# Transposing the gate's columns later, and scaling the first groups at a layer border on one engine

## The chip, the cores and the metric

The kernel runs on one core of a Trainium2 chip. The metric is device time in microseconds (us) of one execution, median of three runs. TensorE (PE) multiplies matrices into eight PSUM banks, VectorE (DVE) and ScalarE (ACT) work element by element, POOL (GpSimd) here issues a few transfers and computes a few powers, SP issues the loads. Each engine takes its instructions strictly in the order of the program; between engines only semaphores order the work.

## The reference

A trunk of two layers on x (256 tokens, 2048 columns), all float32:

```python
cond = silu(c)
for i in range(2):
    mod = cond @ mod_w[i] + mod_b[i]
    shift, scale, gate = split(mod, 3)
    h = rms_norm(x, norm_w[i]) * (1.0 + scale) + shift
    y = mixer(h) @ w_out          # layer 0 ("A"): dilated windows, three head groups; layer 1 ("B"): causal blocks
    x = x + gate * y
return rms_norm(x, final_norm_w)
```

Each mixer projects h with a large weight matrix (10 x 2048 columns in A, 4 x 2048 in B), runs attention over 16 heads and multiplies by silu of a part z.

## The kernel before, in words

**Products.** A float32 product is done in three passes of a faster format: every operand is split into a high and a low half, and high x high, high x low and low x high are added in PSUM. The activations are split once (tiles hA, hB, yA, yB: index 0 the high half, index 1 the low one). Weights arrive in units of 128 x 1024 (512 KB) in one of five raw tiles; `convert` (L337) issues the load on SP and has ScalarE write the high half wh (L347), and `finish_converts` (L351) has VectorE write the low half wl (L353). Four units fit in the ring of converted tiles; a few more are "held" in other tiles around the border.

**Order.** The order of the work is written out by hand as a list of steps. A step is one call that emits matmuls. `at_once(i, f)` puts f right behind the matmuls of step i; then `finish_converts` emits the low halves of all converted units that still lack them; then come the conversions planned for the step (`plan_conversions`, L357: a unit converts at the step that frees its buffer, and no earlier than eight steps ahead of its first use); then what `at(i, f)` put there:

```python
    for i, (n, pe) in enumerate(steps):
        pe()
        for f, a in first_tasks.get(i, []):
            f(*a)
        finish_converts()
        for m in plan.get(i, []):
            convert(m)
        for f, a in tasks.get(i, []):
            f(*a)
```

**Parts.** The projections run by parts of 512 columns (four heads), 8 units each. A part with the weights stationary (`whole_part`, L535) has twelve steps: four head steps for units 0 and 1 (called h0 to h3 in the text), one step each for units 2, 3, 4 and 5, and four head steps for units 6 and 7, after each of which a head is moved from PSUM by ScalarE and VectorE (L547, L548). In a head step and in every second step the low-half products (L302) and the high ones (L297) change order. Behind the last head of a part z ScalarE also takes the silu, with a table load (L550).

**The gate.** The vector `mod` is computed by VectorE, 512 columns of `mod_w` at a time (`mod_unit`, L135, L143: multiply by cond and sum), spread over the steps by `add_pieces` (L171). For the gate third of a layer (part 2) it ends with `gate_write` at step i1 + 1, where i1 is the step after the last piece: `mod_sums` (L149) adds four partial sums for each of 16 columns, TensorE transposes the 16 columns (L161) into a PSUM bank (ps_y), ScalarE copies them (L163), POOL writes them to DRAM (L164). `gate_read` at i1 + 3 has POOL read them back, spread over all partitions, into the tiles `gate` (L169). In both layers i1 is the first step, h0, of the part behind a part z.

**The border of the layers.** The out product of layer A ends with column group 3, first for token tile 0 (last step `mid`), then in eight more steps for tile 1 (last step `last`). Behind each of the two, `epilogue` (L679) gates and adds (L684, L686) and sums squares (L691) on VectorE, POOL takes the power (L703), and `norm_b` (L718) has VectorE write a diagonal (L721). `norm_transpose(tt, g)` (L723) then transposes four blocks of group g with the diagonal on TensorE (L728) and scales them: VectorE the first n blocks into hf (L736), ScalarE the others into hs (L738), with n = 3 for even g and 2 for odd g. `norm_split` (L741) writes the high halves on ScalarE (L194) and the low ones on VectorE (L195), one instruction each for hf and for hs. Groups 0 to 3 of tile 0 are transposed at steps mid + 3, 5, 9 and 11, those of tile 1 at last + 4, 5, 6 and 8. Layer B's first part starts at step last + 1 with units 0 to 3 (held) and needs group g from its units 2g and 2g + 1 on, tile 0 first. The conversions of its units 4 and 5 are planned at mid + 5 and mid + 6, so that their low halves come at mid + 6 and mid + 7, which are the steps last - 2 and last - 1.

Of the kernel before, what the change touches and what calls it, by code (L numbers as in the profile page):

```python
# [12 lines left out]
F32 = mybir.dt.float32  # L13
# [5 lines left out]
P = 128  # L19
# [34 lines left out]
def trunk_kernel(ctx: ExitStack, tc: tile.TileContext, x, c, small_w, mod_t, weights, final_norm_w, dmask, out, laid_out):  # L54
# [11 lines left out]
    tmpp = pool("tmpp", 1)  # L66
# [79 lines left out]
    def mod_sums(m, n, step=1):  # L146

        cols = slice(m, m + (n - 1) * step + 1, step)
        nc.vector.tensor_reduce(modc[:, cols], modq[:, cols], axis=AX.X, op=ALU.add)  # L149
# [5 lines left out]

    def gate_write(layer):

        mod_sums(48 * layer + 32, 16)
        scratch[layer] = dram.tile([KC, P], F32, name=f"gate_rows{layer}", tag=f"g{layer}")
        pt = ps_y.tile([P, 512], F32, name="pgt", tag="y")  # L160
        nc.tensor.transpose(pt[:KC, :P], modc[:, 48 * layer + 32:48 * layer + 48], ident)  # L161
        rows = small.tile([P, P], F32, name="grows", bufs=1)
        nc.scalar.activation(rows[:KC], pt[:KC, :P], AF.Copy)  # L163
        nc.gpsimd.dma_start(scratch[layer], rows[:KC])  # L164
# [6 lines left out]
    def add_pieces(i0, i1, layer, part):  # L171

        for n in range(32):
            at(i0 + n * (i1 - i0) // 32, mod_unit, layer, 16 * part + n // 2, n % 2)
        if part == 2:
            at(i1 + 1, gate_write, layer)
            at(i1 + 3, gate_read, layer)

    def scale_b():
        mod_sums(48, 32)  # L180
# [10 lines left out]
    def split(dst, src):  # L191

        hi = dst[:, :, 0]
        nc.scalar.activation(hi, src, AF.Copy)  # L194
        nc.vector.tensor_tensor(dst[:, :, 1], src, hi.bitcast(F32), op=ALU.subtract)  # L195
# [115 lines left out]
    def add_unit(w, u, n0, hold=None, after=-1):  # L311
        return add_halves([(w, 2 * u, n0), (w, 2 * u + 1, n0)], hold, after)
# [6 lines left out]
    def add_step(ns, pe):  # L319
        i = len(steps)  # L320
        steps.append((ns, pe))
        for n in ns if isinstance(ns, tuple) else (ns,):
            if units[n]["first"] is None:
                units[n]["first"] = i
            units[n]["last"] = i
        return i

    def at(i, f, *a):
        tasks.setdefault(i, []).append((f, a))

    def at_once(i, f, *a):

        first_tasks.setdefault(i, []).append((f, a))
# [17 lines left out]
    def finish_converts(c=slice(0, 2)):  # L351
        for raw, wh, wl in to_finish:
            nc.vector.tensor_tensor(wl[:, c], raw[:, c], wh[:, c].bitcast(F32), op=ALU.subtract)  # L353
        if c.stop == 2:
            to_finish.clear()
# [166 lines left out]
    def product(p, key, st, n, u, first, last):  # L522
        def pe():
            moving(group_ps(key), st, (2 * u, 2 * u + 1), conv[n], (0, 1), first, last)
        return add_step(n, pe)
# [58 lines left out]
    while min(done) < KC:  # L584
        n_ready = sum(r <= t for r in READY)
        n = done.index(min(done)) if n_ready < KC else next(i for i, d in enumerate(done) if d < KC)
# [18 lines left out]
    for k in range(1, KC):  # L605
        i0, i1 = READY[k - 1], READY[k]
# [8 lines left out]
    for j in range(1, 4):  # L615
# [4 lines left out]
        for n, p in enumerate(PARTS[EARLY:] if j == 1 else PARTS):  # L620
# [3 lines left out]
            for u in range(8):  # L624
                m = add_unit(wA, u, COL[p] * D + j * GC)
                i = product(p, ("A", j, p), st_a, m, u, u == 0, u == 7)
# [4 lines left out]
    for n, (layer, part) in enumerate(((0, 2), (1, 0), (1, 1))):  # L631
        add_pieces(*(span[0] + (n + k) * (span[1] - span[0]) // 3 for k in range(2)), layer, part)
# [3 lines left out]
    def out_steps(l, w, epilogue, hold):  # L636
        st = lambda kc: ys[l, kc // 4][:, kc % 4]

        def step(g, u, n=None, tts=(0, 1)):
            n = add_unit(w, u, g * GC) if n is None else n  # L640

            def pe():
                moving(group_ps(("o", l, g)), st, (2 * u, 2 * u + 1), conv[n], tts, u == 0, u == 7)
            return add_step(n, pe)

        b0 = len(steps)
        for g in range(2):
            for u in range(6):
                step(g, u)
        for u in (6, 7):  # L650
            for g in range(2):
                i = step(g, u)
                if u == 7:
                    at_once(i, epilogue, g, (0, 1))
        for u in range(8):
            i = step(2, u)
        at_once(i, epilogue, 2, (0, 1))
        b1 = len(steps) + 2
        both = 0 if hold else 4
        for u in range(both):  # L660
            step(3, u)
        ns = {u: add_unit(w, u, 3 * GC, HOLD[u] if hold and u < 4 else None, b0 + 12 if hold else -1) for u in range(both, 8)}
        for u in range(both, 8):
            mid = step(3, u, ns[u], (0,))
        for tt in range(2):
            at(b1, sums_before, tt)
        at_once(mid, epilogue, 3, (0,))
        for u in range(both, 8):
            i = step(3, u, ns[u], (1,))
        at_once(i, epilogue, 3, (1,))  # L670
        return b0, mid, i
# [7 lines left out]
    def epilogue(l):  # L679
        def f(g, tts):  # L680
            ps = groups["o", l, g]
            tmp = tmpp.tile([P, 2, GC], F32, name="tmp", tag="tmp")
            for tt in tts:
                nc.vector.tensor_tensor(tmp[:, tt], ps[tt], gate_of(g), op=ALU.mult)  # L684
            for tt in tts:
                nc.vector.tensor_tensor(X[g][:, tt], X[g][:, tt], tmp[:, tt], op=ALU.add)  # L686
                s = ssp[:, tt * 4 + g:tt * 4 + g + 1]
                if g < 3:
                    nc.scalar.activation(tmp[:, tt], X[g][:, tt], AF.Square, accum_out=s)
                else:  # L690
                    nc.vector.tensor_tensor_reduce(tmp[:, tt], X[g][:, tt], X[g][:, tt], 1.0 / D, ssb[:, tt:tt + 1],  # L691
                                                   ALU.mult, ALU.add, s)
        return f
# [12 lines left out]
    b0, mid, last = out_steps("A", "a_w_out", epilogue("A"), True)  # L706
# [7 lines left out]
    hB_box = []  # L714
# [8 lines left out]
    def norm_transpose(tt, g):  # L723
        if not hB_box:
            hB_box.append(hpool.tile([P, KC, 2, S], F32R, name="hB", tag="h"))
        pt = (ps_s, ps_o, ps_t, ps_y)[g].tile([P, 512], F32, name="pxt", tag="soty"[g])
        for b in range(4):
            nc.tensor.matmul(pt[:, b * P:(b + 1) * P], X[g][:, tt, b * P:(b + 1) * P], rB[tt], start=True, stop=True)  # L728
        hf = tp.tile([P, 4, P], F32, name="t")
        hs = tmpp.tile([P, 2, P], F32, name="hs", tag="tmp")  # L730
        n = 3 - g % 2
        for b in range(4):
            k = 4 * g + b
            src, a, s = pt[:, b * P:(b + 1) * P], abB[:, k:k + 1], modc[:, 48 + k:49 + k]
            if b < n:
                nc.vector.tensor_scalar(hf[:, b], src, a, s, op0=ALU.mult, op1=ALU.add)  # L736
            else:
                nc.scalar.activation(hs[:, b - n], src, AF.Identity, scale=a, bias=s)  # L738
        hfB[tt, g] = (n, hf[:, :n], hs[:, :4 - n])

    def norm_split(tt, g):  # L741
        n, hf, hs = hfB[tt, g]
        split(hB_box[0][:, 4 * g:4 * g + n, :, tt * P:(tt + 1) * P], hf)
        split(hB_box[0][:, 4 * g + n:4 * g + 4, :, tt * P:(tt + 1) * P], hs)

    for tt, i in enumerate((mid, last)):
        at_once(i, norm_b, tt)
        for g, n in enumerate((3, 5, 9, 11) if tt == 0 else (4, 5, 6, 8)):
            at_once(i + n, norm_transpose, tt, g)
            at(i + n, norm_split, tt, g)  # L750
# [3 lines left out]
    for j in range(4):  # L754
# [4 lines left out]
        for p in PARTS_B:  # L759
            col = COL_B[p] * D + j * GC  # L760
            if j == 0 and p == "v":
                ns = [add_unit(wB, u, col, HOLD[u] if u < 4 else None)
                      for u in range(8)]
                for tt in range(2):
                    for u, n in enumerate(ns):
                        def pe(n=n, u=u, tt=tt, key=("B", j, p)):
                            moving(group_ps(key), st_b, (2 * u, 2 * u + 1), conv[n], (tt,), u == 0, u == 7)
                        i = add_step(n, pe)
            elif p != "v":
                i = whole_part("B", j, p, st_b, wB, col)  # L770
                continue
            else:
                for u in range(8):
                    i = product(p, ("B", j, p), st_b, add_unit(wB, u, col), u, u == 0, u == 7)
# [4 lines left out]
    b0, mid, last = out_steps("B", "b_w_out", epilogue("B"), False)  # L779
# [56 lines left out]
    for i, (n, pe) in enumerate(steps):  # L836
        pe()
        for f, a in first_tasks.get(i, []):
            f(*a)
        finish_converts()  # L840
        for m in plan.get(i, []):
            convert(m)
        for f, a in tasks.get(i, []):
            f(*a)
# [38 lines left out]
```

## Time and profile before

| | before |
|---|---|
| median of three runs | 1584.31 us (1582.89 to 1584.82) |
| the profiled execution | 1584.17 us, span of its instructions 1582.1 us |
| mean granted clock of TensorE in the span | 0.994 |
| busy in the span | TensorE 1555.3 us, VectorE 1128.3 us, ScalarE 757.4 us, POOL 30.3 us |
| loads of weights | 512 of 512 KB, on SP's queue |

The span runs from the first to the last instruction; the 2.1 us outside it belong to start and end of the execution. A busy time is the sum of an engine's instructions; matmuls overlap, so a row of several matmuls ends later than the next row starts. "Idle before" is the time an engine stood before an instruction, with the instruction that released it. The granted clock is the share of full speed (2.4 GHz) that TensorE was given, 1.00 or 0.50 at any moment (2.4 or 1.2 GHz).

### The profile page before, as it was taken

How to read it: one execution, taken by the hardware profiler on the slowest of the kernel's cores; microseconds unless marked ns; L12 is line 12 of the kernel's file. 1: busy time of each engine (PE TensorE's matmuls, PEld its weight loads, DVE VectorE, ACT ScalarE, POOL GpSimd, SP SyncE). 2: the span in 40 equal slices, each digit the busy share in tenths (PEclk: the TensorE clock that was granted, in tenths of full speed). 3: DMA queues.
4: the chain of work that ended last, by engine and by line, in shares of the span. 5: the costliest groups of instructions: out<-in, count | busy, mean ns of one | idle time of the engine just before them, and what ended most of it. 6: DMA issues, size and time to landing. Idle time of an engine off the chain costs nothing. (4 is left out here: it accounts for less than half of the span.)

```text
span 1582.1 us, 23691 instructions
## 1 busy us (share of the span) xinstructions
PE 1555.3 (98%) x8960; PEld 1366.4 (86%) x8960; DVE 1128.3 (71%) x2008; ACT 757.4 (48%) x1041; POOL 30.3 (2%) x35
## 2 busy tenths in 40 slices
PE   8999999999999998999999999999999998999997
PEld 6898899999988887888888888888888887888886
DVE  7889887667678766777777775766448887465666
ACT  7644444445444544444544444554545455455542
POOL 4000000000000000000000000000000000000000
PEclk9999999999999999999999999999999999999999
DMA  9978997553788577888578886364467896645543
GB/s 347 344 284 312 317 314 266 189 170 128 236 301 281 187 237 269 303 289 294 205 242 285 294 303 225 129 239 147 135 211 245 295 325 226 213 173 200 187 172 108
DMA packets 104726, 380.77 MB, mean 241 GB/s; under 512 B 11650, under 2 KB 11810, under 8 KB 104356
## 3 DMA queue, kind: packets, MB, share of 16 engines
q1 hardware_dynamic: 102528, 372.95, 67.8%
q0 software_dynamic: 1504, 5.26, 1.0%
q8 instruction: 70, 1.15, 0.3%
q10 hardware_dynamic: 580, 1.06, 0.2%
q14 instruction: 44, 0.36, 0.1%
HBM read 377.10 MB, written 2.11 MB: 240 GB/s over the span
## 5 line engine op out<-in xcount | busy, mean ns | idle before, releaser
L347 ACT ACTIVATE wh<-raw 128x1024 fp32r<-128x1024 f32 (+1 forms) x505 | 527.3, 1056 | 519.1 <-PE acc L297 174.1
L353 DVE TENSOR_TENSOR wl<-raw,wh 128x1024 fp32r<-128x1024 f32 (+1 forms) x505 | 609.0, 1221 | 192.3 <-ACT wh L347 190.8
L297 PE MATMUL acc<-hA,wh 128*128 128x512 f32 x1152 | 289.4, 393 | 0.0
L297 PEld LDWEIGHTS acc<-hA,wh 128*128 128x128 f32 x1152 | 207.8, 189 | 36.7
L297 PE MATMUL acc<-hB,wh 128*128 128x512 f32 x768 | 197.2, 396 | 0.0
L284 PE MATMUL acc<-hA,wh 128*128 128x256 f32 x640 | 182.8, 286 | 1.0 <-ACT hA L256 1.0
L285 PE MATMUL acc<-hA,wh 128*128 128x256 f32 x640 | 182.0, 284 | 0.6 <-DVE hA L262 0.6
L286 PE MATMUL acc<-hA,wl 128*128 128x256 f32 x640 | 181.8, 284 | 0.0
L302 PEld LDWEIGHTS acc<-hA,wl 128*128 128x128 f32 x1152 | 157.8, 191 | 11.8
L302 PE MATMUL acc<-hA,wl 128*128 128x256 f32 x1152 | 161.1, 283 | 0.0
L297 PEld LDWEIGHTS acc<-hB,wh 128*128 128x128 f32 x768 | 138.0, 189 | 23.9
L273 PE MATMUL acc<-wh,hA 128*128 128x512 f32 x384 | 156.0, 406 | 1.0 <-DVE hA L258 1.0
L275 PE MATMUL acc<-wh,hA 128*128 128x512 f32 x384 | 151.1, 394 | 0.4 <-DVE hA L262 0.4
L274 PE MATMUL acc<-wl,hA 128*128 128x512 f32 x384 | 150.6, 392 | 0.0
L143 DVE CUSTOM_DVE_ANT_0 raw<-raw,cb 128x512 f32<-128x512 f32 x198 | 131.1, 689 | 18.4 <-DMA raw<-in_mod_t_dram 18.4
L284 PEld LDWEIGHTS acc<-hA,wh 128*128 128x128 f32 x640 | 123.5, 193 | 1.4 <-ACT hA L256 1.2
L285 PEld LDWEIGHTS acc<-hA,wh 128*128 128x128 f32 x640 | 123.6, 193 | 1.0 <-DVE hA L262 0.8
L286 PEld LDWEIGHTS acc<-hA,wl 128*128 128x128 f32 x640 | 123.5, 193 | 0.0
L302 PEld LDWEIGHTS acc<-hB,wl 128*128 128x128 f32 x768 | 106.0, 191 | 8.6 <-DVE wl L353 0.4
L302 PE MATMUL acc<-hB,wl 128*128 128x256 f32 x768 | 109.0, 284 | 0.2 <-DVE wl L353 0.2
L275 PEld LDWEIGHTS acc<-wh,hA 128*128 128x128 f32 x384 | 72.4, 189 | 17.1 <-DVE hA L262 1.3
L273 PEld LDWEIGHTS acc<-wh,hA 128*128 128x128 f32 x384 | 72.7, 189 | 15.9 <-ACT hf L259 2.2
(235 smaller groups left out, 1780.7 us busy)
## 6 DMA issues: line engine op xcount, KB each, us to landing
raw<-in_weights_dram SPq DMA_DIRECT2D x512, 512.0 KB, 4.4
raw<-in_mod_t_dram SPq DMA_DIRECT2D x132, 512.0 KB, 4.7
gate<-in_mod_t_dram SPq DMA_DIRECT2D x40, 512.0 KB, 5.3
dm<-in_mod_t_dram SPq DMA_DIRECT2D x20, 512.0 KB, 5.3
xin<-in_x_dram SPq DMA_DIRECT2D x2, 1024.0 KB, 6.2
gate<-gate_rows POOLq DMA_DIRECT2D x4, 512.0 KB, 6.9
x<-in_x_dram POOLq DMA_DIRECT2D x4, 512.0 KB, 6.4
fw<-in_final_norm_w_dram POOLq DMA_DIRECT2D x2, 512.0 KB, 4.7
```

Source lines behind the costliest of these rows:

```text
L143: nc.vector.tensor_tensor_reduce(part, part, cb[q], 1.0, 0.0 if q else mbT[:, m:m + 1], ALU.mult, ALU.add, modq[:, m, q:q + 1])
L273: nc.tensor.matmul(o, hi, wh[:, i], start=f, stop=False, skip_group_check=True)
L274: nc.tensor.matmul(o, hi, wl[:, i], start=False, stop=False, skip_group_check=True)
L275: nc.tensor.matmul(o, lo, wh[:, i], start=False, stop=l, skip_group_check=True)
L284: nc.tensor.matmul(o, wh[:, i, wc], hi, start=first and h % 2 == 0, stop=False, skip_group_check=True)
L285: nc.tensor.matmul(o, wh[:, i, wc], lo, start=False, stop=False, skip_group_check=True)
L286: nc.tensor.matmul(o, wl[:, i, wc], hi, start=False, stop=last, skip_group_check=True)
L297: nc.tensor.matmul(ps_of(h), ws[u][0][:, i, cols(h)], both, start=us[u] == 0 and i == 0, stop=low_first and us[u] == 7 and i == 1, skip_gr ...
L302: nc.tensor.matmul(ps_of(h)[:, 0:S], ws[u][1][:, i, cols(h)], st(2 * us[u] + i)[:, 0, :], start=False, stop=not low_first and us[u] == 7 a ...
L347: nc.scalar.activation(wh[:, c], raw[:, c], AF.Copy)
L353: nc.vector.tensor_tensor(wl[:, c], raw[:, c], wh[:, c].bitcast(F32), op=ALU.subtract)
```

## The change

The sums of the gate's columns stay at step i1 + 1. The transpose, the copy and the write move from i1 + 1 to i1 + 8, the read back from i1 + 3 to i1 + 10, in both layers. At the border, for groups 0 and 1 of tile 0, VectorE scales all four blocks, into one tile, and ScalarE none; the split is then one instruction on each engine. At the steps last - 2 and last - 1 no low halves are emitted; they follow at step `last`, behind the gating and the diagonal of tile 1.

```diff
     def gate_write(layer):
 
-        mod_sums(48 * layer + 32, 16)
         scratch[layer] = dram.tile([KC, P], F32, name=f"gate_rows{layer}", tag=f"g{layer}")
...
         if part == 2:
-            at(i1 + 1, gate_write, layer)
-            at(i1 + 3, gate_read, layer)
+            at(i1 + 1, mod_sums, 48 * layer + 32, 16)
+            at(i1 + 8, gate_write, layer)
+            at(i1 + 10, gate_read, layer)
...
         hf = tp.tile([P, 4, P], F32, name="t")
-        hs = tmpp.tile([P, 2, P], F32, name="hs", tag="tmp")
-        n = 3 - g % 2
+        n = 4 if tt == 0 and g < 2 else 3 - g % 2
+        hs = tmpp.tile([P, 2, P], F32, name="hs", tag="tmp") if n < 4 else hf
...
         split(hB_box[0][:, 4 * g:4 * g + n, :, tt * P:(tt + 1) * P], hf)
-        split(hB_box[0][:, 4 * g + n:4 * g + 4, :, tt * P:(tt + 1) * P], hs)
-
+        if n < 4:
+            split(hB_box[0][:, 4 * g + n:4 * g + 4, :, tt * P:(tt + 1) * P], hs)
+
+    late_low = range(last - 2, last)
...
-        finish_converts()
+        if i not in late_low:
+            finish_converts()
```

## Rows read from the trace of the kernel before

**Rows 1.** The page: busy us (share of the span) and instructions of each engine.
```profile
PE 1555.3 (98%) x8960; PEld 1366.4 (86%) x8960; DVE 1128.3 (71%) x2008; ACT 757.4 (48%) x1041; POOL 30.3 (2%) x35
```
**Rows 2.** Waits of TensorE, whole span: waiting, releaser, us, times, longest.
```profile
PE pgt L161 <- DVE modc L149: 9.0, 2, 4.8
...
PE acc L273 <- ACT hB L194: 1.2, 1, 1.2
...
PE acc L302 <- DVE wl L353: 0.2, 1, 0.2
```
**Rows 3.** Timeline of TensorE, first place: start, us, instruction, [idle before].
```profile
601.81 1.09 PE L297 MATMUL acc<-hA,wh 128*128 128x512 f32 x4
...
609.57 0.28 PE L161 MATMUL pgt<-ident,modc 128*16 128x128 f32 x1 [4.80 <-DVE modc L149]
...
614.99 3.82 PE L297 MATMUL acc<-hA,wh 128*128 128x512 f32 x16
...
630.75 1.09 PE L297 MATMUL acc<-hA,wh 128*128 128x512 f32 x4
...
637.33 3.82 PE L297 MATMUL acc<-hA,wh 128*128 128x512 f32 x16
```
**Rows 4.** Timeline of TensorE, second place.
```profile
1332.00 1.08 PE L297 MATMUL acc<-hB,wh 128*128 128x512 f32 x4
...
1344.56 3.82 PE L297 MATMUL acc<-hB,wh 128*128 128x512 f32 x16
...
1360.32 1.09 PE L297 MATMUL acc<-hB,wh 128*128 128x512 f32 x4
...
1366.89 3.82 PE L297 MATMUL acc<-hB,wh 128*128 128x512 f32 x16
```
**Rows 5.** Windows: length, busy of PE, PEld, DVE, ACT, POOL; granted clock, DMA share, GB/s.
```profile
609.60:613.60 4.00, 4.00 (x14) 3.33 (x15) 1.13 (x4) 0.57 (x2) 0.71 (x1) 0.57 0.79 260
1340.10:1344.00 3.90, 3.90 (x18) 3.47 (x17) 0.57 (x1) 1.85 (x2) 0.48 (x1) 0.56 0.42 151
...
617.00:624.00 7.00, 7.00 (x40) 6.08 (x40) 3.95 (x7) 3.19 (x3) 1.10 (x2) 1.00 0.95 310
```
**Rows 6.** Timeline of VectorE at the two places.
```profile
605.74 2.36 DVE L353 TENSOR_TENSOR wl<-raw,wh 128x1024 fp32r<-128x1024 f32 x2 [2.89 <-ACT wh L347]
...
609.30 0.22 DVE L149 TENSOR_REDUCE modc<-modq 128x16 f32<-128x64 f32 x1
...
1336.61 2.36 DVE L353 TENSOR_TENSOR wl<-raw,wh 128x1024 fp32r<-128x1024 f32 x2 [2.83 <-ACT wh L347]
```
**Rows 7.** The page: DMA issues, count, KB each, median us from issue to landing.
```profile
raw<-in_weights_dram SPq DMA_DIRECT2D x512, 512.0 KB, 4.4
...
gate<-gate_rows POOLq DMA_DIRECT2D x4, 512.0 KB, 6.9
```
**Rows 8.** Timeline of VectorE at the border.
```profile
1081.81 1.05 DVE L736 TENSOR_SCALAR t<-pxt,abB,modc 128x128 f32<-128x128 f32 x3 [0.64 <-PE pxt L728]
...
1084.82 0.56 DVE L195 TENSOR_TENSOR hB<-t,hB 128x384 fp32r<-128x384 f32 x1 [0.83 <-ACT hB L194]
...
1089.57 0.43 DVE L195 TENSOR_TENSOR hB<-t,hB 128x256 fp32r<-128x256 f32 x1 [1.08 <-ACT hB L194]
...
1090.25 2.35 DVE L353 TENSOR_TENSOR wl<-raw,wh 128x1024 fp32r<-128x1024 f32 x2
1092.52 0.68 DVE L684 TENSOR_TENSOR tmp<-acc,gate 128x512 f32<-128x512 f32 x1
...
1095.39 0.29 DVE L721 TENSOR_SCALAR diag<-ident,rstd 128x128 f32<-128x128 f32 x1 [0.66 <-POOL rstd L703]
...
1096.73 1.04 DVE L736 TENSOR_SCALAR t<-pxt,abB,modc 128x128 f32<-128x128 f32 x3
```
**Rows 9.** Timeline of TensorE at the border.
```profile
1089.33 0.39 PE L273 MATMUL acc<-held,hB 128*128 128x512 f32 x1
...
1098.81 0.50 PE L273 MATMUL acc<-wh,hB 128*128 128x512 f32 x1 [1.17 <-ACT hB L194]
```

## The prediction, made before the change was timed

> **What bounds the kernel now.** I read the page's busy times first: the matmuls fill 1555.3 of the 1582.1 us span, VectorE 71% and ScalarE 48% [rows 1]. So a change is worth what it takes from TensorE's order of work or adds to it, and the next view is the list of what TensorE waited for. The largest entry by far is 9.0 us in two waits, of 4.8 and (the rest) 4.2 us, of the gate's transposes for the sums of L149; the only wait at the border of the layers is 1.2 us for a high half of hB; low halves of weights (L353) cost 0.2 us in the whole span [rows 2]. The timeline of each place tells what a wait costs beyond its idle time, the granted clock tells why, and VectorE's timeline tells what was late.
>
> **Part 1: the transposes go seven steps later, the sums stay.** VectorE reaches the sums late because they are queued behind two low halves, which wait for ScalarE. At the first place these start at 605.74 and the sums at 609.30; at the second the low halves start at 1336.61 [rows 6]. TensorE, which is in order, stands at the transpose with ready heads behind it.
>
> What goes, first place. From the start of step h0 (601.81) to the first high product of unit 2 (614.99) are 13.18 us. The next part does the same work without the transpose from 630.75 to 637.33, in 6.58 us [rows 3]. So 6.60 us go: the 4.80 idle, 0.2 around the transpose, and 1.6 of slow products behind it, for the granted clock is 0.57 over the 4.00 us after the wait, which is full speed falling to the half level and back [rows 5]. Second place: 1332.00 to 1344.56 is 12.56 us, against 1360.32 to 1366.89, 6.57 [rows 4]: 5.99 us go, 4.2 of them idle, with the clock at 0.56 over 3.90 us behind it [rows 5]. Together 12.59 us, some 3.2 of which are clock.
>
> The Trainium skill ("TensorE: Matmul & The Clock Gate", section Terms) prices slow stretches by a rule: throttled time multiplied by one minus the granted share. By it the two stretches would cost 4.00 x 0.43 + 3.90 x 0.44 = 3.4 us and the whole sum would be 0.2 us larger. The trace is a little below that, as steps bound by something else lose less, and the measured difference stands in my sum.
>
> What takes its place. At the new step (i1 + 8, the first head step of units 6 and 7) PE's next wait could again be for the sums. Without the stall that step ends at about 604.6 + 2 x 1.4 + 4 x 2.8 + 1.4 = 620.0 (1.40 a head step, 2.8 a unit, from the spacing of [rows 3]); the sums are there by 609.5 [rows 6], ten us before. The transposes themselves still run: nothing to 0.28 us each (0.28 is the whole row [rows 3]; the next product started 0.04 behind it); I take 0.1, as matmuls overlap: 0.2 for both.
>
> What is late next: unit 2, whose low half is used first. First place: h2 and h3 now end at 607.4; the first of the two low halves, 1.2 us long, is done at 606.9 [rows 6]: no wait, 0.5 to spare. Second place: PE arrives at 1332.00 + 4 x 1.40 = 1337.6, the low half is done at 1336.61 + 1.2 = 1337.8, so a new wait of 0.25 us; the 0.2 us already in the waits is of this kind [rows 2]. Unit 3 comes 2.8 us after unit 2 and its low half 1.1. Units 4 and 5 convert once h3 has freed their buffers; those steps move forward with PE. Their loads are the doubt: SP issues a load when VectorE frees one of five raw tiles, and a load takes 4.4 us to land [rows 7]. Unit 5's raw tile is freed by unit 2's low half at 606.9, so it lands at about 611.4 and is converted by 613.6; PE wants it at 615.8. Unit 7's lands some 2.5 us after it and PE wants it at 618.6: a us or so to spare.
>
> Other queues moved past. ScalarE's copy of the transposed rows (L163) now sits between two evacuations of heads, where it idles; POOL's write and re-read have POOL's queue to themselves there, and the gate is read first by the gating of the out product, which for the first place is the row at 1092.52 and its kind, over 400 us later [rows 8]. I cost these at nothing; if their cover went, it would be DMA time, below as a rival. Part 1: 12.59 - 0.25 - 0.2 = **12.1 us**.
>
> **Part 2: the border.** TensorE waits 1.17 us at 1098.81 for the high half of group 2, tile 0 [rows 9]. That group was transposed early, but VectorE scales it only at 1096.73 [rows 8]: it was busy with low halves until 1092.52, then gating until the diagonal at 1095.39, then one more low half. Yet the last out product ended at 1089.33 [rows 9]. I place the new order in a row from 1081.81, in durations of [rows 8]: 4 scalings (1.05 / 3 each) 1.40, low half 1.2, one merged split of 512 columns 0.7 (0.56 for 384), low half 1.2, 4 scalings 1.4, low half 1.2, split 0.7: 1089.6. ScalarE's high halves come inside this, since it no longer has three scalings waiting for VectorE. The idle 0.83 and 1.08 us of VectorE at 1084.82 and 1089.57 are filled. So the gating starts at 1089.6 instead of 1092.52, 2.9 us earlier, and the diagonal at 1092.45. But then the two postponed low halves (2.27) run with the third one ahead of group 2: 1092.45 + (1096.73 - 1095.39) + 2.27 = 1096.06, only 0.7 us earlier. The wait shrinks from 1.17 to 0.5. The postponed halves themselves (units 4 and 5) are done at 1093.8 and 1094.9, and TensorE wants unit 4's just after 1098. What this part can do at most is remove 1.17; at worst the five us of extra or later VectorE work cost what they add, 3 x 0.35 = 1.05 less 0.2 of merged splits: 0.85 us lost. I take **+0.7**, because the idle that absorbs the added work is in the rows.
>
> **Sum.** 12.1 + 0.7 = 12.8 us off the profiled execution's 1584.17 (span 1582.1 and 2.1 around it), so 1571.4; the median of the three runs, 1584.31, is 0.14 above the profiled one, within their scatter of 1.9.
>
> **Rivals.**
> (a) *Weights late, once.* The gate's re-read is 2 x 0.5 MB and now falls in a busy stretch instead of behind a stall in which loads had got ahead. At 310 GB/s [rows 5] it takes 3.4 us of DMA time. If the first place passes that on to TensorE (a unit's spare time above is about 1 us), the result is 1571.4 + 3.4 = 1574.8. For: five raw tiles only, and 4.4 us to land. Against: from 617 to 624, where the re-read ran before, the DMA engines were 0.95 busy and TensorE 7.00 of 7.00 [rows 5]. At the second place the share was 0.42, so only one is counted. 12 in 100.
> (b) *Slower.* The same re-read, place i1 + 10, not sharing but going first: two issues of 6.9 us each [rows 7], 13.8 us without weights. With half of the four converted units in hand (2 x 2.8 us) TensorE would stand for 8.2 us, and lose 1.6 to the clock, at both places: 19.6 lost against 12.8 gained, about 1591. It decides once each place loses over 8 us. Against: again the stretch from 617 to 624. 2 in 100.
> The Trainium skill ("Trainium Kernel Development and Optimization", Key Constraints) speaks for (a) over (b): transfers issued from SP, ScalarE and POOL use the same 16 DMA engines and interleave. The trace agrees at 617 to 624, where both kinds were in flight and neither stopped TensorE.
> (c) *The change does not do what it says:* the moved transpose waits again, for its bank or a later VectorE instruction, as long as before. Then only the border is left: 1583.5. Against: the wait's releaser is L149 itself [rows 2]. 3 in 100.
> (d) *The clock falls anyway* at both places, although the idle is gone: 3.2 us less, 1574.6. Against: the drop is seen only behind the wait. 3 in 100.
>
> **The numbers.** The forecast has the other 80 in 100. Its own bounds: border wholly gone, no new wait and no cost of the transposes, clock by the rule, 0.5 + 0.25 + 0.2 + 0.2 better, less a us of scatter: 1569.4. At the other end the border loses 0.85 instead of gaining 0.7 and a us of scatter: 1574; (a) and (d) bring it to 1575.0. A difference under 0.2% (3.2 us) is about what a measurement of this kernel can't tell from none. Faster 0.95 (forecast, a, d), same 0.03 (c), slower 0.02 (b).
>
> **What would show it.** TensorE's waits without pgt, or under 0.1; L161 some 15 us behind L149; no half clock behind it; h0 to unit 2's high products 6.6 us at the first place, 6.8 at the second; a wait for a low half of some 0.25 at the second; at the border the gating at about 1089.6 and the wait for hB near 0.5. Wrong would be: new waits for wh or wl in the two parts behind the places (a, b), pgt still in the waits (c), a half clock without a wait (d), or a gating that starts past 1091.

## The result, and the profile after

The changed kernel takes 1573.1 us (median of four, 1571.62 to 1573.42) against 1584.31: a ratio of 0.9929, 95% interval 0.9912 to 0.9946. That is 11.2 us faster; 1571.4 was forecast, with a range of 1569.4 to 1575.0. The profiled execution took 1571.62 us, its span is 1569.6.

The page's first part, after (it answers to [rows 1]): TensorE's busy time fell by 4.9 us although it does the same matmuls, since fewer of them run at the half clock.

```profile
PE 1550.4 (99%) x8960; PEld 1361.2 (87%) x8960; DVE 1129.1 (72%) x2009; ACT 756.2 (48%) x1036; POOL 30.2 (2%) x35
```

TensorE's waits, after (to [rows 2]): pgt is gone from the list. A wait for a low half of 1.7 us is new, and the one for hB is 0.4 instead of 1.2.

```profile
PE acc L302 <- DVE wl L353: 1.7, 1, 1.7
...
PE acc L273 <- ACT hB L194: 0.4, 1, 0.4
```

TensorE's timeline at the first place, after (to [rows 3]): h0 starts at 600.11, unit 2's high products at 606.69, the moved transpose runs at 618.64 without a wait, and the new wait stands at 635.95.

```profile
600.11 1.09 PE L297 MATMUL acc<-hA,wh 128*128 128x512 f32 x4
...
606.69 3.82 PE L297 MATMUL acc<-hA,wh 128*128 128x512 f32 x16
...
615.91 1.97 PE L302 MATMUL acc<-hA,wl 128*128 128x256 f32 x12
617.72 1.09 PE L297 MATMUL acc<-hA,wh 128*128 128x512 f32 x4
618.64 0.27 PE L160 MATMUL pgt<-ident,modc 128*16 128x128 f32 x1
...
635.95 1.22 PE L302 MATMUL acc<-hA,wl 128*128 128x256 f32 x8 [1.67 <-DVE wl L353]
```

The same at the second place, after (to [rows 4]).

```profile
1324.97 1.08 PE L297 MATMUL acc<-hB,wh 128*128 128x512 f32 x4
...
1330.10 1.98 PE L302 MATMUL acc<-hB,wl 128*128 128x256 f32 x12
1331.91 3.82 PE L297 MATMUL acc<-hB,wh 128*128 128x512 f32 x16
```

From h0 to unit 2's high products are now 6.58 us (13.18 before) and 6.94 us (12.56 before): 6.60 and 5.62 us went. Windows of the kernel after show full speed behind the first place (to [rows 5]), and also at 97 us, where the profiled execution of before had a half clock:

```profile
606.00:620.00 14.00, 13.88 (x80) 11.94 (x79) 11.28 (x22) 5.94 (x8) 0.33 (x1) 1.00 0.92 310
...
97.00:101.00 4.00, 4.00 (x35) 4.00 (x35) 4.00 (x9) 1.06 (x1) 0.00 (x0) 1.00 0.91 325
```

The window of before for that stretch:

```profile
97.80:101.30 3.50, 3.50 (x19) 3.50 (x18) 3.25 (x7) 0.93 (x1) 0.00 (x0) 0.51 0.75 231
```

Nothing that runs there was changed, so 1.7 us of the two spans' difference belong to the two executions (h0 of the first place starts at 600.11 instead of 601.81). The 12.5 us between the spans are: 1.7 at the start, 6.60 and 5.62 at the two places, 0.73 at the border, less 1.67 for the new wait and 0.38 at 615.91, where twelve low-half products take 1.81 us to the next start instead of 1.43. These add up to 12.6, or to 12.3 with the new wait's price by distance (1.93, worked out at the end of the experiments). Without the start, about 10.8 us of the 12.5 are the change's, and the medians say 11.2.

VectorE's timeline at the border, after (to [rows 8]):

```profile
1075.91 1.37 DVE L736 TENSOR_SCALAR t<-pxt,abB,modc 128x128 f32<-128x128 f32 x4 [0.64 <-PE pxt L728]
...
1083.63 0.69 DVE L684 TENSOR_TENSOR tmp<-acc,gate 128x512 f32<-128x512 f32 x1 [0.47 <-PE acc L275]
...
1086.71 3.49 DVE L353 TENSOR_TENSOR wl<-raw,wh 128x1024 fp32r<-128x1024 f32 x3
1090.12 1.04 DVE L736 TENSOR_SCALAR t<-pxt,abB,modc 128x128 f32<-128x128 f32 x3
```

The gating starts 7.72 us behind the first scalings (10.71 before, [rows 8]), 3.0 us earlier, and group 2's scaling 14.21 behind them (14.92 before), 0.7 earlier. VectorE itself was ready 7.25 us behind the first scalings; it then stood 0.47 for the end of the last out product.

Where the new wait of 1.67 us comes from, in VectorE's timeline after: it stands 5.30 us at a load of `mod` columns (issued on SP at 625.76, so over 7 us on the way), and the low halves that TensorE waits for are queued behind it.

```profile
633.39 0.75 DVE L143 CUSTOM_DVE_ANT_0 raw<-raw,cb,smalls 128x512 f32<-128x512 f32 x1 [5.30 <-DMA raw<-in_mod_t_dram]
...
634.68 4.63 DVE L353 TENSOR_TENSOR wl<-raw,wh 128x1024 fp32r<-128x1024 f32 x4
```

And POOL's timeline after: the gate's re-read was issued at 625.07, just ahead of that load.

```profile
625.07 1.10 POOL L168 DMA_DIRECT2D gate<-gate_rows  x2 [4.69 <-DVE actA2q L548]
```

That is the prediction's rival (a) in kind, at about half its price. At the second place, where the re-read goes out too (POOL, 1347.95), no such wait came. The experiments ask whether the re-read is its cause (theory 1) or the loads run short there anyway (theory 2), what the clock costs, and which of the two border edits does the work.

### The profile page after: what moved, and what is told of

It is laid out like the page before. It is cut to its first block, busy times and chain, and to the rows that moved or that the text cites. A ratio compares the mean times of both kernels' runs of the same rounds, so it can differ in the third digit from the quotient of the medians.

```text
span 1569.6 us, 23684 instructions
## 1 busy us (share of the span) xinstructions
PE 1550.4 (99%) x8960; PEld 1361.2 (87%) x8960; DVE 1129.1 (72%) x2009; ACT 756.2 (48%) x1036; POOL 30.2 (2%) x35
## 4 chain that ended last, share of the span: by engine, by line
PE 91%; DVE 1%; DMA 1%; issue 0%; ACT 0%; POOLq 0%; POOL 0%; DVEq 0%; ACTq 0%
PE acc L297 27%; PE acc L302 14%; PE acc L273 11%; PE acc L275 11%; PE acc L274 10%; PE acc L285 4%; PE acc L286 4%; PE acc L284 4%; PE po L461 2%; PE pss L443 2%; PE pst L424 1%; DMA raw<-in_mod_t_dram 1%; PE po L494 1%; PE pss L478 1%; DVE wl L353 1%
```

## The experiments

Short diffs are against the changed kernel, or against the one before where that is said. Comparisons by profile are made by waits and distances, because whether and where a half clock falls in the first 100 us differs from execution to execution.

**The gate part alone.**

```diff
-        n = 4 if tt == 0 and g < 2 else 3 - g % 2
+        n = 3 - g % 2
...
-    late_low = range(last - 2, last)
+    late_low = range(0)
```

> The change with the border as it was before (scaling shared, low halves not postponed); the gate's transposes stay at i1 + 8. If the border part is worth the 0.7 us that the prediction gave it: the wait of the first products behind the border for hB is back at 1.1 to 1.2 us (0.44 with the whole change), everything at the two gate places as with the whole change (no pgt wait, one wait for a low half of about 1.7 us some 35 us behind the first place), time about 1573.8 us. If the border part is worth nothing: the wait stays near 0.4 and the time at 1573.1. If it did more than shorten that wait: over 1575.

Measured: 1573.04 us (ratio to before 0.9935, interval 0.9919 to 0.9951). TensorE's waits in this run:

```profile
PE acc L302 <- DVE wl L353: 2.0, 2, 1.8
PE acc L273 <- ACT hB L194: 1.2, 1, 1.2
```

The border's wait is back in full, as expected. Times can't tell 0.7 us here; the waits can. The new wait behind the first place (1.80, the longer of the two) comes with the gate part.

**The border part alone** (transposes at i1 + 1, read at i1 + 3, the rest as changed).

> The kernel before with the border part alone; the transposes stay at i1 + 1. If the parts are independent: pgt waits of 9.0 us as before, half clock behind both, the hB wait at 0.4 instead of 1.17, the gating of tile 1 within 0.3 us of the end of the last out product, span 0.7 us under before's (1581.4 where the clock does the same at the start). If the border is bound by something else: the hB wait above 0.9.

Measured: one run of 1581.9 us, span 1579.8; pgt 9.0 us in two waits, hB 0.44. The parts are independent. The span is 2.3 us under before's instead of 0.7, of which 1.7 lie ahead of the first place's stage (the first whole part starts at 404.8 us instead of 406.5; no half clock near 97 us in this execution either).

**Layer 0's gate read back later.**

```diff
-            at(i1 + 10, gate_read, layer)
+            if layer:
+                at(i1 + 10, gate_read, layer)
...
+    at(b0 + 3, gate_read, 0)
     at(b0 - 10, load_x, 0)
```

> The whole change, but layer 0's gate is read back only at the fourth step of the out product of layer A, some 360 us later, where no mod loads run. Theory 1, the re-read of 1 MB delays the loads (a mod load lands late, VectorE stands at it, the low half behind it is late): the wait of 1.7 us for a low half some 35 us behind the first place goes, all of it, no other wait above 0.5 us comes near the first place, the gate's sums and transposes as before; 1571.4 us. Theory 2, the loads run short behind the first place because the stall in which they got ahead is gone, re-read or not: a wait of over 1 us for a low half stays within 50 us behind the first place; 1573.1. If the out product has no room for the re-read: a new wait for a weight between steps b0 and b0 + 10.

Measured: 1570.66 us (1569.27 to 1571.5; ratio 0.992, interval 0.9902 to 0.9938). No wait for a low half is left in TensorE's whole list. In this kernel's timeline VectorE stands 2.10 us at the `mod` load instead of 5.30:

```profile
629.73 0.75 DVE L143 CUSTOM_DVE_ANT_0 raw<-raw,cb,smalls 128x512 f32<-128x512 f32 x1 [2.10 <-DMA raw<-in_mod_t_dram]
```

This is theory 1's outcome: without the re-read the load is on its way 4.4 us instead of 7.6 (issued at 625.30 here) and is there 3.2 us sooner, about what 1 MB takes at the 310 GB/s of the window above (3.4 us, an estimate). Theory 2 is not without ground, though: even here VectorE stands 2.10 us at this load and 1.39 at an earlier one (614.35), and the twelve low-half products at 615.47 take 1.78 us to the next start (1.81 with the re-read, 1.43 before). The loads run short behind the first place with or without the re-read; without it the shortage stays inside the slack. One thing in the expectation was wrong. POOL's timeline shows the read not at the out product but some 175 us after the write (619.22), right behind two loads of x:

```profile
792.41 1.50 POOL L678 DMA_DIRECT2D x<-in_x_dram  x2 [172.49 <-DVE wl L354]
793.91 1.10 POOL L168 DMA_DIRECT2D gate<-gate_rows  x2
```

POOL is busy for 2% of the span and here runs ahead of the steps: its load of x waits for a low half of VectorE by the profile, and the read follows at once. There 2 MB came together and TensorE did not wait (10.00 us busy of the 10 from 794, at a DMA share of 0.99). The share had been 0.62 from 780 to 790, against 0.90 to 1.00 in each four us from 610 to 626 in the kernel after.

**Four steps instead of seven later** (`gate_write` at i1 + 4, `gate_read` at i1 + 6).

> The whole change with the transposes at i1 + 4 and the read at i1 + 6 instead of 8 and 10. The sums are there about 2.5 us before that step ends at either place, so no pgt wait (under 0.1). Theory 1: the re-read now meets other loads, some 8 us earlier; the wait some 35 us behind the place goes or shrinks, and one of 0 to 2 us may come 10 to 25 us behind it; time 1571.4 to 1573.4. Theory 2: the wait of 1.7 us stays where it was. If seven steps were needed: pgt waits of over 1 us.

Measured: 1570.96 us (ratio 0.992, interval 0.9904 to 0.9936), no pgt wait, so seven steps are not needed. But the wait for a low half is where it was, 1.63 us, with the read issued at 617.88, 7 us earlier. In TensorE's timeline:

```profile
608.60 0.27 PE L160 MATMUL pgt<-ident,modc 128*16 128x128 f32 x1
...
635.62 1.21 PE L302 MATMUL acc<-hA,wl 128*128 128x256 f32 x8 [1.63 <-DVE wl L353]
```

Theory 1 as I had put it expected the wait to move with the read. It didn't: by the letter this is theory 2's outcome. I read that as the DMA engines being full here (0.92 over the 14 us from 606 in the kernel after), so that a delay is handed on from load to load until one is too late; that is argued and not shown. Shown is that the place within this stretch matters little, and that leaving the stretch does away with the wait. The medians don't tell the two runs apart: 1570.96 with the wait here, 1570.66 without it in the run with the late read. Nor does the profile explain why this median is 2.1 us under the changed kernel's: the spans are 1569.3 and 1569.6. The mean granted clock was 0.996 in the changed kernel's three other executions, 0.998 in its profiled one and 0.997 to 0.998 here, so one more stretch at the half clock would be of the right size; where it lay no trace shows.

**Two steps and three steps** (`gate_write` at i1 + 2 and at i1 + 3, the read two steps behind).

> The whole change with the transposes at i1 + 2 (one step later than before; read at i1 + 4). The sums come as before, so the idle at the transposes is 4.8 - 1.4 = 3.4 us at the first place and 4.2 - 1.4 = 2.8 at the second. If the clock falls behind any such wait: half clock behind both, 1.6 us each on top. If only the longer waits before made it fall: no half clock, and a step costs its idle time alone.

> The same at i1 + 3 (read at i1 + 5): idle 2.0 us at the first place, 1.4 at the second. If the clock's cost goes with the idle time, 0.6 us each of slow products behind them; if it is all or nothing, a half clock of the same length as before (1.6 us lost) or none. At i1 + 4 there was no wait, so the number of steps that the move needs is 3 at each place, not 7.

Measured: 1579.57 us with two steps and 1574.33 with three, one run each. The idle times are 3.40 and 2.80 us with two steps, 2.00 and 1.40 with three, to 0.1 us as the spacing of the steps said. TensorE's waits, first with two steps, then with three:

```profile
PE pgt L160 <- DVE modc L149: 6.2, 2, 3.4
PE pgt L160 <- DVE modc L149: 3.4, 2, 2.0
```

Windows behind the two waits with two steps:

```profile
608.00:615.00 7.00, 7.00 (x27) 6.12 (x28) 3.50 (x6) 2.33 (x4) 0.71 (x1) 0.61 0.91 287
1336.00:1340.00 4.00, 4.00 (x19) 3.73 (x20) 2.13 (x2) 2.27 (x3) 0.56 (x1) 0.63 0.71 246
```

and with three, followed by TensorE's timeline at the first place:

```profile
609.60:613.60 4.00, 4.00 (x22) 3.50 (x23) 3.41 (x6) 2.12 (x3) 0.71 (x1) 1.00 0.89 269
1333.70:1337.70 4.00, 4.00 (x22) 3.48 (x23) 2.18 (x2) 1.42 (x3) 0.56 (x1) 1.00 0.82 287
```
```profile
601.81 1.09 PE L297 MATMUL acc<-hA,wh 128*128 128x512 f32 x4
...
609.58 0.28 PE L160 MATMUL pgt<-ident,modc 128*16 128x128 f32 x1 [2.00 <-DVE modc L149]
...
610.65 3.82 PE L297 MATMUL acc<-hA,wh 128*128 128x512 f32 x16
```

The clock's price was not in proportion to the idle time: a half clock came behind 2.8, 3.4, 4.2 and 4.8 us, and how long it lasted varied (0.61 over 7.00 us behind the 3.4); behind 1.4 and 2.0 there was none. With three steps the distance from h0 to unit 2's high products is 8.84 us at the first place (601.81 to 610.65), 2.26 over the undisturbed 6.58: the idle time and 0.26. So the step from two to three is worth more than a step of idle time. With three steps there was also no wait for a low half behind the first place, although the re-read went out at 617.88, 16.1 us behind h0 (17.7 with four steps, where the wait came). The difference is the 2 us of stall that are left, which gave the loads their time. So the new wait needed both: the re-read in this stretch, and a stall all but gone.

**The two border edits one by one**, each in the kernel before: only n = 4, then only the late low halves.

> The kernel before with VectorE alone scaling groups 0 and 1 of tile 0; low halves not postponed, transposes at i1 + 1 as before. Theory S (the gain at the border is VectorE's filled idle time, and the postponing makes VectorE stand until the last out product ends): the hB wait is under 0.2 us, less than the 0.44 of the whole change, as two low halves fill that gap. Theory L (the gain is the earlier gating): the hB wait is 0.9 to 1.2.

> The kernel before with the two low halves behind the last tile's gating and nothing else (scaling shared as before, transposes at i1 + 1). Theory S: gating 2 us earlier, group 2's scaling at the same time, the hB wait stays at 1.0 to 1.3 us. Theory L: the hB wait falls to 0.6 or less.

Measured, one run each (1581.95 and 1582.86 us): with the scaling alone no wait for hB at all; with the postponing alone 1.35 us, more than the 1.17 of before and a little over theory S's range. VectorE's timeline with the scaling alone, in which it has no idle time between the first scalings and the gating:

```profile
1081.17 1.37 DVE L736 TENSOR_SCALAR t<-pxt,abB,modc 128x128 f32<-128x128 f32 x4 [0.64 <-PE pxt L728]
...
1088.34 2.35 DVE L353 TENSOR_TENSOR wl<-raw,wh 128x1024 fp32r<-128x1024 f32 x2
1090.61 0.68 DVE L684 TENSOR_TENSOR tmp<-acc,gate 128x512 f32<-128x512 f32 x1
...
1094.82 1.04 DVE L736 TENSOR_SCALAR t<-pxt,abB,modc 128x128 f32<-128x128 f32 x3
```

and with the postponing alone, where the gating starts early and group 2's scaling late:

```profile
1080.36 1.05 DVE L736 TENSOR_SCALAR t<-pxt,abB,modc 128x128 f32<-128x128 f32 x3 [0.64 <-PE pxt L728]
...
1088.98 0.69 DVE L684 TENSOR_TENSOR tmp<-acc,gate 128x512 f32<-128x512 f32 x1
...
1092.06 3.49 DVE L353 TENSOR_TENSOR wl<-raw,wh 128x1024 fp32r<-128x1024 f32 x3
1095.47 1.04 DVE L736 TENSOR_SCALAR t<-pxt,abB,modc 128x128 f32<-128x128 f32 x3
```

From the first scalings to those of group 2 are 14.92 us before, 13.65 with the scaling alone, 15.11 with the postponing alone and 14.21 with both. The postponed low halves stand ahead of group 2 in either order, so an earlier gating gains nothing for it; and while VectorE waits for the last out product (0.47 us in the whole change) it could have done them. Theory S holds.

**The read twice.**

```diff
             at(i1 + 10, gate_read, layer)
+            if layer == 0:
+                at(i1 + 10, gate_read, layer)
```

> The whole change, but layer 0's gate is read back twice at i1 + 10 (2 MB instead of 1 MB on POOL's queue). If the DMA engines' time is what is short there (theory 1): TensorE's waits for low halves in the 60 us behind the first place grow from 1.7 by about the time of one more re-read, 3 to 4 us, to 4.5 to 5.5 us. If the wait is a matter of the loads' order and not of the bytes: it stays below 2.5 us.

Measured: 1573.99 us, one run. Of three waits for low halves the first lies ahead of the read (626.77); behind it are 1.9 us, not the 4.5 to 5.5 that theory 1 wanted. TensorE's timeline:

```profile
619.32 0.51 PE L304 MATMUL acc<-hA,wl 128*128 128x256 f32 x2 [0.32 <-DVE wl L355]
637.73 1.22 PE L304 MATMUL acc<-hA,wl 128*128 128x256 f32 x8 [1.50 <-DVE wl L355]
655.18 1.22 PE L304 MATMUL acc<-hA,wl 128*128 128x256 f32 x8 [0.42 <-DVE wl L355]
```

The second read was not beside the first but behind it: its halves went out at 634.73 and 637.21, once the first had landed. Behind it came 0.42 us, at 655. So a megabyte more does not cost a fixed time; but the run did not do what was meant, two reads at the same time, and can't decide what that would cost. I read the small price as a question of whether the tiles in hand cover the delay, which is argued and not shown. Why the idle is 1.5 to 2.2 us for the first read and 0.4 for one 8 to 10 us later stays open.

**Both improvements together, beside the changed kernel again.** The read late as above, `late_low` taken out:

```diff
-    late_low = range(last - 2, last)
...
-        if i not in late_low:
-            finish_converts()
+        finish_converts()
```

> The whole change without the two postponed low halves, and with layer 0's gate read back at the fourth step of the out product. If the parts add up: no wait for hB at the border (0.44 in the whole change), no wait of 1.7 us behind the first place, all else as in the whole change: 2.1 us under the whole change, about 1571.0 against 1573.1 (run beside it here). If they don't: the border wait comes back because TensorE's order there has moved, 0.4 us or more.

> The whole change once more, unaltered, beside the other two on the same chip: 1573.1 us by the first measurement, within 1; the wait of 1.6 to 1.8 us for a low half behind the first place in its profile again, if it belongs to the program and not to one execution.

Measured on the same chip, against a before of 1582.72 us: both together 1569.74 us (1568.96 to 1570.87; ratio 0.9917, interval 0.9904 to 0.9931); the changed kernel 1574.59 (1572.5 to 1575.3; ratio 0.9944, interval 0.9931 to 0.9958). The version with both is 4.8 us under the changed kernel, and no run of either overlaps the other's range. TensorE's list has neither the wait for hB nor the long one for a low half. Expected were 2.1 us; the changed kernel itself came out 1.5 us above its first median, where 1 was allowed. There the changed kernel gains 8.1 us on the kernel before, against 11.2 the first time. A part of the rest shows in the changed kernel's second profile: its wait was 2.16 us this time, and a half clock followed (another one stood near 97 us). TensorE's timeline and the window behind the wait:

```profile
631.05 3.82 PE L297 MATMUL acc<-hA,wh 128*128 128x512 f32 x16
...
637.98 1.21 PE L302 MATMUL acc<-hA,wl 128*128 128x256 f32 x8 [2.16 <-DVE wl L353]
...
657.38 3.82 PE L297 MATMUL acc<-hA,wh 128*128 128x512 f32 x16
```
```profile
639.00:643.00 4.00, 4.00 (x13) 3.15 (x12) 3.01 (x6) 0.59 (x1) 0.00 (x0) 0.57 0.90 306
```

and TensorE's timeline over the same products in the kernel after:

```profile
629.51 3.82 PE L297 MATMUL acc<-hA,wh 128*128 128x512 f32 x16
...
653.77 3.82 PE L297 MATMUL acc<-hA,wh 128*128 128x512 f32 x16
```

From unit 2's high products to those of the next part is 22.34 us where nothing waits (614.99 to 637.33 in [rows 3]), 24.26 in the kernel after and 26.33 here. So the new wait costs 1.9 us in an execution like the first, and 4.0 in one like this.

## Why the prediction was right

- **The transposes' wait and its clock.** 12.59 us were to go; 6.60 and 5.62 went, the second less a new wait. The transposes run unwaited for, about 11 us behind their sums (607.61 and 618.64). That 3.2 us of it are the clock's was argued from the distances and is borne out by the run with three steps: idle without a half clock cost the idle and 0.26. The prediction's sign "some 15 us" behind the sums did not follow from its own working (620.0 less 609.5 is 10.5); 11.0 came. And the ground given against rival (d), that the drop is seen only behind the wait, left out the third half clock of the kernel before, at 97.8 to 101.3 us.
- **What is late next.** Unit 2's low half at the second place was to cost 0.25; the distance there is 6.94 against 6.57 undisturbed, 0.37. Unit 7 at the first place was given "a us or so to spare" and came 0.38 us late. The 0.2 us of before that the prediction took for unit 2's kind is of unit 7's: it lies at 1253.30, in the first head step of units 6 and 7.
- **The step that failed: "I cost these at nothing", of POOL's write and re-read.** With the stall gone, the re-read costs 1.6 to 2.2 us of waiting, in one profile of four with a half clock on top (kernel after, gate part alone, four steps, changed kernel again). The forecast had it as rival (a), at 12 in 100 and 3.4 us for all its DMA time. That the re-read brings it was shown by moving the read away: the load was there 3.2 us sooner then, near the rival's 3.4. TensorE had paid 1.67 to 1.93 of them; that tiles in hand covered the rest is argued. My argument against (a), that TensorE never waited from 617 to 624 before, was misread: those loads had been given the stall's five us, and the stall was what the change removed. The run with three steps shows it: same re-read, 2 us of stall left, no wait.
- **The border.** 0.7 us was forecast and 0.73 came, by the sum's own steps (early gating, three low halves, group 2). The start of the gating, 7.79 us behind the first scalings by the sum and 7.72 measured, agrees partly by luck: VectorE was ready at 7.25, and the end of the out product set the start. But the sum was for both edits at once and hid that they pull opposite ways: the scaling alone removes the whole 1.17, the postponing gives 0.44 back. The text's bound of 1.17 was reachable by doing less.
- **The total.** 12.8 us were forecast, 11.2 came by the medians (10.8 between the profiles without their start, 8.1 by the medians of the second occasion). The wait behind the first place and unit 7's 0.38 are the size of the difference in the profiles. The range's lower bound is added up wrongly: its terms give 1569.2 and not 1569.4. Without rivals (a) and (d) its upper end was 1574, and the second occasion's 1574.59 would have been outside.

## What to carry to other kernels

When a stall is taken out of an engine that sets the time, list what else used its time: here the loads got ahead in it, and a transfer that had been free behind it became the next wait. Move such a transfer to where the DMA share is lower, and check in the profile where it is really issued: POOL here ran ahead of the written order. And price the edits of a pair one by one: filling an engine's idle time and reordering it to start something earlier can cancel.

## What was not expected of the hardware

The granted clock did not follow the idle time in any simple way. It halved behind waits of 2.8 us and more in every execution seen, stayed at full speed behind 1.4 and 2.0, and behind waits of 1.5 to 1.8 (the new wait in four profiles) as well, but halved behind 2.16. At about 97 us, behind waits of 1.01 and 0.57 us that are the same in both first profiles, it halved in one execution and not in the other; it did so in five of the thirteen profiles. The medians of the same kernel on two occasions, 1573.1 and 1574.6, differ by about what one such stretch costs (1.6 us at the first place).
